# Pair blocks of the MLP: one transfer of four blocks, the first combination in place, and products in program order

## The chip, the cores and the metric

The kernel runs on one core of a Trainium2 chip. A core has a matrix engine (TensorE, PE in the profile; its weight loads are PEld), a vector engine (VectorE, DVE), an activation engine (ScalarE, ACT), a general engine (GpSimd, POOL), and a sync engine (SyncE, SP) that here only issues transfers. Each engine works through its own instructions in order and waits on semaphores for the others. Sixteen DMA engines move data. Weights come from the device memory (HBM) into the on-chip memory SBUF; TensorE adds up its products in PSUM, which has eight banks of 128 x 512 float32.

The metric is the device time of one execution in microseconds. Runs are compared by their median, and the profile is of one execution.

## What is computed

A two-layer encoder over 256 tokens of width 2048. Each layer is: normalisation, token mixing in heads, output projection, and an MLP. What the change touches is the MLP:

```python
n = rms_norm(h, mlp_norm[i])
h = h + jnp.square(jax.nn.relu(n @ w_up[i])) @ w_down[i]
```

`w_up` is 2048 x 8192 and `w_down` 8192 x 2048, all float32. TensorE works on float32r operands, so every weight tile is split into a high part (written by ScalarE) and the residual low part (VectorE subtracts). A product of two split operands is high x high, high x low and low x high: three matrix products.

## The kernel before

**Grains.** The MLP is a list of grains (`add_mlp`, line 969). A grain has a `run` (its products on TensorE), an `after`, and up to three earlier stages: `load`, `pre`, `prep`. `run_all` (line 274) walks the list; before it runs grain n it issues the loads of grains up to n + 8, the `pre` of those up to n + 5 and the `prep` of those up to n + 4 (`SOON`, line 964). This is the program order. A scheduler then orders each engine's instructions by its own estimate; instructions given to `pin` keep their program order among each other.

**Up.** The hidden width is cut into 8 parts of 8 blocks of 128. For one block (`up_grains`, line 749, two grains), SyncE loads 1 MiB of `w_up` into `raw_U`, ScalarE and VectorE split it in two halves into `uh` and `ul` (line 329 and 330), and `u_products` (line 727) makes 48 products of 256 columns into one PSUM tile `ps_u`. `squared` (line 782) then applies the ReLU (line 789) and the square (line 790) on ScalarE into `c`. For every second block VectorE forms four combinations (line 799), and the seven operands are split into `a_s`. Part 0 runs by itself; its `ps_u` tiles rotate through the four banks of the pool `ps_acc`.

**Down, by pairs.** For parts 0 to 6 the product with `w_down` is made for pairs: two hidden blocks of 128 and two column blocks of 512 at a time, with seven products in place of eight (a Strassen-like scheme with the sums p1 to p7). There are 56 such steps in a layer (`down_grains`, line 806), each beside one hidden block of the next part. The four 128 x 512 blocks of a pair come as 1024 KB: three go into tile `b` (line 814, 768 KB), the fourth into the first place of tile `t` (line 816, 256 KB). Then:

- `pre`: VectorE writes t[1] = t[0] + b[0] (line 828), and GpSimd issues a DMA that adds b[1] onto t[0] in place (line 829).
- `prep_first`: `b` (1536 columns) is split into `bh` and `bl`.
- `prep_second`: VectorE writes t[2] = t[1] + b[1] and t[3] = t[2] + b[2] (lines 837 and 838), and `t` (2048 columns) is split into `th` and `tl`.
- `run`: the products of `FIRST` (three sums, 9 products of 512 columns) use `bh` and `bl`; those of `SECOND` (four sums, 12 products) use `th` and `tl`.

`b` and `t` have two buffers each, `bh`, `bl`, `th` and `tl` one each. The seven sums stay in PSUM for eight steps at a time; when a half of the columns ends, `taken` (line 885) adds them to `h` (line 883) or to `z` (line 894), and at two places per layer `folded` combines `z` into `h`.

**PSUM.** All eight banks are in use. The pools `ps_acc` and `ps_att` (four banks each) are closed before the pairs and a pool `ps_sums` is opened, with one bank for the hidden block (tag `up`) and one for each sum. This happens in the first hidden block of part 1 (lines 763 to 768); the sums take their banks in the order p4, p3, p1, p2, p5, p7, p6 (line 871). After the pairs the pools change back.

**Plain.** Part 7 is multiplied without pairs (`plain_grains`, line 914): 1 MiB loads that alternate between the buffers with tag `U` and those with tag `T`, splits, and products into `ps_m` of `ps_acc`.

**Order of the list.** Behind part 0, each step adds four grains: first half of the hidden block, first half of the pair, second half of the hidden block, second half of the pair (line 976).

Of the kernel before, what the change touches and what calls it, by code (L numbers as in the profile page):

```python
# [10 lines left out]
F32 = mybir.dt.float32  # L11
F32R = mybir.dt.float32r
BF16 = mybir.dt.bfloat16
AF = mybir.ActivationFunctionType
ALU = mybir.AluOpType
# [75 lines left out]
def encoder_kernel(ctx: ExitStack, tc: tile.TileContext, t: dict, out: bass.AP):  # L91
# [632 lines left out]
    FIRST = ("p3", 6, 0), ("p1", 0, 1), ("p2", 2, 2)  # L724
    SECOND = ("p5", 3, 0), ("p7", 4, 1), ("p6", 5, 2), ("p4", 1, 3)

    def u_products(ps, k0, nk, hi, lo):

        acts = box["hT"]
        for j in range(nk):  # L730
            k = k0 + j
            s = slice(j * P, (j + 1) * P)
            parts = (slice(0, SEQ), slice(SEQ, 512))
            for n, x in enumerate(parts if k < KT - 1 else parts[::-1]):
                nc.tensor.matmul(ps, hi[:, s], acts[:, k, x], start=k == n == 0, stop=False)  # L735
            nc.tensor.matmul(ps, lo[:, s], acts[:, k, :SEQ], start=False, stop=k == KT - 1)  # L736
# [12 lines left out]
    def up_grains(layer, part, m):  # L749
# [8 lines left out]
        def run(hf):  # L758
            if hf == 0:
                if part == 0:  # L760
                    own["ps"] = at.acc.tile([P, 512], F32, tag="acc", name="ps_u")[:, :SEQ]
                else:
                    if part == 1 and m == 0:
                        closed("ps_att", "ps_acc")
                        at.sums = opened("ps_sums", space=bass.MemoryType.PSUM)
                        box["ps"] = {}
                        box["unused"] = set()
                    own["ps"] = at.sums.tile([P, 512], F32, tag="up", name="ps_u")[:, :SEQ]
            u_products(own["ps"], hf * (KT // 2), KT // 2, *own.pop(hf))
# [36 lines left out]
    def down_grains(layer, part, n, begins, ends):  # L806
# [4 lines left out]
        def load():  # L811
            src = t[f"w_pair{layer}"][(part * 2 + q) * STEPS + j]
            own["b"] = at.side.tile([P, 3 * 512], F32, tag="b", bufs=2, name="b")
            nc.sync.dma_start(own["b"], src[:, : 3 * 512])
            own["t"] = at.side.tile([P, 4, 512], F32, tag="T", bufs=2, name="t")
            nc.sync.dma_start(own["t"][:, 0, :], src[:, 3 * 512 :])
# [5 lines left out]
        def block(k):  # L822

            return own["b"][:, k * 512 : (k + 1) * 512]

        def pre():
            s = own["t"]
            nc.vector.tensor_tensor(s[:, 1, :], s[:, 0, :], block(0), op=ALU.add)  # L828
            nc.gpsimd.dma_start(s[:, 0, :], block(1), accum_op=ALU.add)  # L829

        def prep_first():
            own["first"] = tuple(at.mlp.tile([P, 3 * 512], F32R, tag=x, name=x) for x in ("bh", "bl"))
            split(*own["first"], own["b"])

        def prep_second():
            s = own["t"]
            nc.vector.tensor_tensor(s[:, 2, :], s[:, 1, :], block(1), op=ALU.add)
            nc.vector.tensor_tensor(s[:, 3, :], s[:, 2, :], block(2), op=ALU.add)
            own["second"] = tuple(at.mlp.tile([P, CH], F32R, tag=x, name=x) for x in ("th", "tl"))
            split(*own["second"], s.rearrange("p a b -> p (a b)"))  # L840

        def run(which, products):
            hi, lo = own.pop(which)
            a = box["a", part, j]
            for name, ai, bi in products:
# [3 lines left out]
                nc.tensor.matmul(ps, a[:, 0, ai, :], hi[:, s], start=begins, stop=False)  # L849
# [64 lines left out]
    def plain_grains(layer, nb):  # L914
# [6 lines left out]
        def load(c):  # L921
            own[c] = loaded(t[f"w_plain{layer}"][nb * 2 + c], "UT"[c])
# [46 lines left out]
    def add_mlp(layer):  # L969
        for m in range(PK):  # L970
            plan.extend(up_grains(layer, 0, m))
        for x, (p, n) in enumerate(STEPS_OF):
# [3 lines left out]
            plan.extend((up[0], down[0], up[1], down[1]))  # L976
# [304 lines left out]
```

## Time and profile before

| | |
|---|---|
| median of 3 runs | 2047.32 us (2046.8 to 2050.19) |
| the profiled execution | 2048.19 us |
| its span, first to last instruction | 2046.4 us |
| busy: PE / PEld / DVE / ACT / POOL | 2026.7 / 1813.8 / 1667.0 / 1251.6 / 119.2 us |
| read from HBM, mean | 398.17 MB, 197 GB/s |
| loads of pair blocks | 112 of 768 KB, 112 of 256 KB |

How to read the profile's lines: a group line names the source line, the engine, the operation, output<-inputs, shape and count, then busy time in us, mean ns of one, and the engine's idle time just before these instructions with what ended it. A line of a wait list gives who waited <- for whom: us in total, times, the longest. A line of the stage table gives the stretch in us from the start, its length, the busy time (and instructions) of each engine, the granted clock of PE as a share of full speed, the DMA engines' mean busy share, and GB/s. A timeline line gives the start, the duration, the instruction, and in brackets the engine's idle time before it and what released it. Lines of transfers give count, size and the median time from issue to landing. Matmul ends are modelled and overlap, so the distance between two starts is what a matmul costs.

### The profile page before, as it was taken

The numbers are of one execution on the slowest core, as the hardware profiler recorded it, in microseconds if no ns is written. First come the engines' busy times: TensorE is split into PE (matmuls) and PEld (weight loads), VectorE is DVE, ScalarE is ACT, GpSimd is POOL, SyncE is SP. The second block draws the span as 40 slices with busy tenths as digits, with TensorE's granted clock in tenths as the row PEclk, the third lists the DMA queues.
The fourth block names the chain that finished last, engine by engine and source line by source line (L and its number), as shares of the span: only waits on it lengthen the run. The fifth ranks groups of instructions, "written<-read, shape, count | busy, mean of one in ns | idle before, by whom it ended". The sixth has DMA issues, their size and how long they took to land.

```text
span 2046.4 us, 31582 instructions
## 1 busy us (share of the span) xinstructions
PE 2026.7 (99%) x12516; PEld 1813.8 (89%) x12516; DVE 1667.0 (81%) x2061; ACT 1251.6 (61%) x1652; POOL 119.2 (6%) x144
## 2 busy tenths in 40 slices
PE   8999999999999999999999999999999999999998
PEld 7888888889999999999988888889999999999996
DVE  6767667558989989999897667657998989999996
ACT  6755555556666666666656557556666666666664
POOL 0000000000000000000000001000000000000000
PEclk9999999999999999999999999999999999999999
DMA  7755554727777777787775554536877777777773
GB/s 281 283 190 179 191 177 169 277 80 233 231 231 232 220 232 230 226 242 222 230 222 199 180 185 144 184 125 216 246 227 227 227 231 229 234 232 227 236 221 130
DMA packets 93429, 433.79 MB, mean 212 GB/s; under 512 B 10464, under 2 KB 12128, under 8 KB 60128
## 3 DMA queue, kind: packets, MB, share of 16 engines
q1 hardware_dynamic: 75456, 398.47, 57.3%
q0 software_dynamic: 16816, 31.46, 8.7%
q8 instruction: 98, 1.61, 0.3%
q10 hardware_dynamic: 1008, 1.84, 0.3%
q14 instruction: 51, 0.42, 0.1%
HBM read 398.17 MB, written 4.19 MB: 197 GB/s over the span
## 4 chain that ended last, share of the span: by engine, by line
PE 93%; DVE 3%; DMA 2%; issue 1%; ACT 0%; POOLq 0%; POOL 0%; SPq 0%; DVEq 0%; ACTq 0%
PE ps_u L735 21%; PE ps_u L736 11%; PE ps_m L234 8%; PE ps_m L237 8%; PE ps_m L238 8%; PE p L849 8%; PE p L850 8%; PE p L851 8%; PE ps_s L247 7%; PE ps_s L250 3%; DMA t<-in_w_pair 1%; DVE tl L330 1%; PE pt_a L410 1%; DVE ul L330 1%; PE pt_n L347 1%
## 5 line engine op out<-in xcount | busy, mean ns | idle before, releaser
L735 PE MATMUL ps_u<-hT,uh 128*128 128x256 f32 x4096 | 713.2, 278 | 0.2
L735 PEld LDWEIGHTS ps_u<-hT,uh 128*128 128x128 f32 x4096 | 627.4, 188 | 10.3 <-ACT uh L329 0.6
L736 PE MATMUL ps_u<-hT,ul 128*128 128x256 f32 x2048 | 568.9, 278 | 1.6 <-DVE ul L330 1.5
L329 ACT ACTIVATE uh<-raw_U 128x1024 fp32r<-128x1024 f32 x278 | 294.6, 1061 | 307.1 <-PE ps_u L735 290.0
L330 DVE TENSOR_TENSOR lo<-raw,hi 128x1024 fp32r<-128x1024 f32 (+1 forms) x220 | 261.4, 1194 | 164.5 <-ACT hi L329 162.9
L736 PEld LDWEIGHTS ps_u<-hT,ul 128*128 128x128 f32 x2048 | 386.2, 189 | 4.2 <-DVE ul L330 3.2
L330 DVE TENSOR_TENSOR ul<-raw_U,uh 128x1024 fp32r<-128x1024 f32 x278 | 337.3, 1218 | 40.6 <-ACT uh L329 40.5
L329 ACT ACTIVATE hi<-raw 128x1024 fp32r<-128x1024 f32 (+1 forms) x220 | 227.5, 1039 | 210.2 <-PE ps_m L238 119.1
L329 ACT ACTIVATE th<-t 128x2048 fp32r<-128x2048 f32 x112 | 215.2, 1921 | 118.7 <-PE p L851 107.8
L330 DVE TENSOR_TENSOR tl<-t,th 128x2048 fp32r<-128x2048 f32 x112 | 256.0, 2286 | 23.9 <-ACT th L329 23.5
L330 DVE TENSOR_TENSOR bl<-b,bh 128x1536 fp32r<-128x1536 f32 x112 | 196.0, 1750 | 0.3 <-ACT bh L329 0.3
L850 PE MATMUL p<-tl,a_s 128*128 128x512 f32 x448 | 174.8, 390 | 0.0
L851 PE MATMUL p<-th,a_s 128*128 128x512 f32 x448 | 174.3, 389 | 0.0
L329 ACT ACTIVATE bh<-b 128x1536 fp32r<-128x1536 f32 x112 | 166.2, 1484 | 7.3 <-PE p L851 1.2
L829 POOL DMA_DIRECT2D t<-b x112 | 97.0, 866 | 1158.8 <-DVE t L828 556.0
L849 PE MATMUL p<-th,a_s 128*128 128x512 f32 x448 | 164.1, 391 | 0.0
L247 PE MATMUL ps_s<-nT,hi 128*128 128x512 f32 x448 | 142.5, 397 | 0.0
L851 PE MATMUL p<-bh,a_s 128*128 128x512 f32 x336 | 131.1, 390 | 0.0
L850 PE MATMUL p<-bl,a_s 128*128 128x512 f32 x336 | 131.0, 390 | 0.0
L828 DVE TENSOR_TENSOR t<-t,b 128x512 f32<-128x512 f32 x112 | 77.2, 689 | 57.6 <-DMA t<-in_w_pair 46.5
L849 PE MATMUL p<-bh,a_s 128*128 128x512 f32 x336 | 108.0, 389 | 0.0
L237 PE MATMUL ps_m<-lo,nT 128*128 128x512 f32 x264 | 103.7, 393 | 0.0
(237 smaller groups left out, 3305.1 us busy)
## 6 DMA issues: line engine op xcount, KB each, us to landing
raw_U<-in_w_up SPq DMA_DIRECT2D x128, 1024.0 KB, 6.6
b<-in_w_pair SPq DMA_DIRECT2D x112, 768.0 KB, 4.5
raw<-in_w_o SPq DMA_DIRECT2D x32, 1024.0 KB, 5.0
t<-in_w_pair SPq DMA_DIRECT2D x112, 256.0 KB, 3.4
t<-b POOLq DMA_DIRECT2D x112, 256.0 KB, 6.9
raw<-in_w_b SPq DMA_DIRECT2D x21, 1024.0 KB, 4.9
raw<-in_w_av SPq DMA_DIRECT2D x12, 1024.0 KB, 4.9
raw<-in_w_aq SPq DMA_DIRECT2D x12, 1024.0 KB, 4.9
```

Source lines behind the costliest of these rows:

```text
L234: first = nc.tensor.matmul(w.ps[i], ah, hi[:, s], start=st, stop=False)
L237: nc.tensor.matmul(w.ps[i], ah, lo[:, s], start=False, stop=False)
L238: nc.tensor.matmul(w.ps[i], al, hi[:, s], start=False, stop=sp)
L247: nc.tensor.matmul(ps, hi[:, s], acts[:, k0 + j, :], start=k0 + j == 0, stop=False)
L329: first = nc.scalar.activation(dst_hi, src, AF.Copy)
L330: return first, nc.vector.tensor_tensor(dst_lo, src, dst_hi.bitcast(F32), op=ALU.subtract)
L735: nc.tensor.matmul(ps, hi[:, s], acts[:, k, x], start=k == n == 0, stop=False)
L736: nc.tensor.matmul(ps, lo[:, s], acts[:, k, :SEQ], start=False, stop=k == KT - 1)
L829: nc.gpsimd.dma_start(s[:, 0, :], block(1), accum_op=ALU.add)
L849: nc.tensor.matmul(ps, a[:, 0, ai, :], hi[:, s], start=begins, stop=False)
L850: nc.tensor.matmul(ps, a[:, 0, ai, :], lo[:, s], start=False, stop=False)
L851: nc.tensor.matmul(ps, a[:, 1, ai, :], hi[:, s], start=False, stop=ends)
```

## The change

- The four blocks of a pair come in one transfer of 1024 KB into `b`, which now has four places (two buffers, as before). `t` has three places and is written by VectorE only; it is taken in `pre`.
- The fourth block, raw, sits in b[3]. VectorE writes t[0] = b[3] + b[0]; GpSimd's DMA then adds b[1] onto b[3] in place. The other two additions move from `prep_second` to `pre`.
- `prep_first` splits the four places of `b` (2048 columns), `prep_second` the three of `t` (1536). The sum p5 moves from `SECOND` to `FIRST`, so the groups have 12 and 9 products.
- In the list of a step the pair's first grain comes ahead of the hidden block's first grain. The closing of the old PSUM pools and the opening of `ps_sums` move from the hidden block to the first grain of the first pair.
- The first product of each group of three is pinned: in `u_products` (from part 1 on) and in the pair's `run`. Among themselves these keep their program order on TensorE.
- The plain stage's second load uses the buffers with tag `b` in place of `T`.

```diff
-    FIRST = ("p3", 6, 0), ("p1", 0, 1), ("p2", 2, 2)
-    SECOND = ("p5", 3, 0), ("p7", 4, 1), ("p6", 5, 2), ("p4", 1, 3)
+    FIRST = ("p3", 6, 0), ("p1", 0, 1), ("p2", 2, 2), ("p5", 3, 3)
+    SECOND = ("p7", 4, 0), ("p6", 5, 1), ("p4", 1, 2)
...
-    def u_products(ps, k0, nk, hi, lo):
+    def u_products(ps, k0, nk, hi, lo, keep_order=False):
...
-                nc.tensor.matmul(ps, hi[:, s], acts[:, k, x], start=k == n == 0, stop=False)
+                first = nc.tensor.matmul(ps, hi[:, s], acts[:, k, x], start=k == n == 0, stop=False)
+                if keep_order and n == 0:
+                    pin(first)
...
                 else:
-                    if part == 1 and m == 0:
-                        closed("ps_att", "ps_acc")
-                        at.sums = opened("ps_sums", space=bass.MemoryType.PSUM)
-                        box["ps"] = {}
-                        box["unused"] = set()
                     own["ps"] = at.sums.tile([P, 512], F32, tag="up", name="ps_u")[:, :SEQ]
-            u_products(own["ps"], hf * (KT // 2), KT // 2, *own.pop(hf))
+            u_products(own["ps"], hf * (KT // 2), KT // 2, *own.pop(hf), keep_order=part > 0)
...
         def load():
-            src = t[f"w_pair{layer}"][(part * 2 + q) * STEPS + j]
-            own["b"] = at.side.tile([P, 3 * 512], F32, tag="b", bufs=2, name="b")
-            nc.sync.dma_start(own["b"], src[:, : 3 * 512])
-            own["t"] = at.side.tile([P, 4, 512], F32, tag="T", bufs=2, name="t")
-            nc.sync.dma_start(own["t"][:, 0, :], src[:, 3 * 512 :])
+            own["b"] = at.side.tile([P, 4, 512], F32, tag="b", bufs=2, name="b")
+            nc.sync.dma_start(own["b"].rearrange("p a b -> p (a b)"),
+                              t[f"w_pair{layer}"][(part * 2 + q) * STEPS + j])
...
         def pre():
-            s = own["t"]
-            nc.vector.tensor_tensor(s[:, 1, :], s[:, 0, :], block(0), op=ALU.add)
-            nc.gpsimd.dma_start(s[:, 0, :], block(1), accum_op=ALU.add)
+
+            b, s = own["b"], at.side.tile([P, 3, 512], F32, tag="T", bufs=2, name="t")
+            nc.vector.tensor_tensor(s[:, 0, :], b[:, 3, :], b[:, 0, :], op=ALU.add)
+            nc.gpsimd.dma_start(b[:, 3, :], b[:, 1, :], accum_op=ALU.add)
+            nc.vector.tensor_tensor(s[:, 1, :], s[:, 0, :], b[:, 1, :], op=ALU.add)
+            nc.vector.tensor_tensor(s[:, 2, :], s[:, 1, :], b[:, 2, :], op=ALU.add)
+            own["t"] = s
...
         def prep_first():
-            own["first"] = tuple(at.mlp.tile([P, 3 * 512], F32R, tag=x, name=x) for x in ("bh", "bl"))
-            split(*own["first"], own["b"])
+            own["first"] = tuple(at.mlp.tile([P, CH], F32R, tag=x, name=x) for x in ("bh", "bl"))
+            split(*own["first"], own["b"].rearrange("p a b -> p (a b)"))
...
         def prep_second():
-            s = own["t"]
-            nc.vector.tensor_tensor(s[:, 2, :], s[:, 1, :], block(1), op=ALU.add)
-            nc.vector.tensor_tensor(s[:, 3, :], s[:, 2, :], block(2), op=ALU.add)
-            own["second"] = tuple(at.mlp.tile([P, CH], F32R, tag=x, name=x) for x in ("th", "tl"))
-            split(*own["second"], s.rearrange("p a b -> p (a b)"))
+            own["second"] = tuple(at.mlp.tile([P, 3 * 512], F32R, tag=x, name=x) for x in ("th", "tl"))
+            split(*own["second"], own["t"].rearrange("p a b -> p (a b)"))
...
         def run(which, products):
+            if part == n == 0 and which == "first":
+                closed("ps_att", "ps_acc")
+                at.sums = opened("ps_sums", space=bass.MemoryType.PSUM)
+                box["ps"] = {}
+                box["unused"] = set()
...
-                nc.tensor.matmul(ps, a[:, 0, ai, :], hi[:, s], start=begins, stop=False)
+                pin(nc.tensor.matmul(ps, a[:, 0, ai, :], hi[:, s], start=begins, stop=False))
...
-            own[c] = loaded(t[f"w_plain{layer}"][nb * 2 + c], "UT"[c])
+            own[c] = loaded(t[f"w_plain{layer}"][nb * 2 + c], "Ub"[c])
...
-            plan.extend((up[0], down[0], up[1], down[1]))
+            plan.extend((down[0], up[0], up[1], down[1]))
```

More of the change, by code (lines that the diff above doesn't have):

```diff
@@ L818, in behind @@
         def behind(fn):
             return (lambda: past(fn, box["splits"][-4])) if part == 0 and n < 2 else fn
-        def block(k):
-            return own["b"][:, k * 512 : (k + 1) * 512]
         def pre():
-            s = own["t"]
-            nc.vector.tensor_tensor(s[:, 1, :], s[:, 0, :], block(0), op=ALU.add)
-            nc.gpsimd.dma_start(s[:, 0, :], block(1), accum_op=ALU.add)
+            b, s = own["b"], at.side.tile([P, 3, 512], F32, tag="T", bufs=2, name="t")
+            nc.vector.tensor_tensor(s[:, 0, :], b[:, 3, :], b[:, 0, :], op=ALU.add)
```

## The prediction

> **What bounds the kernel now.** I read the page's first two parts, then the busy times by stage, then the waits of TensorE (PE), and last two short stretches of the timeline.
>
> ```profile
> span 2046.4 us, 31582 instructions
> PE 2026.7 (99%) x12516; PEld 1813.8 (89%) x12516; DVE 1667.0 (81%) x2061; ACT 1251.6 (61%) x1652; POOL 119.2 (6%) x144
> ```
> ```profile
> core 0: us, PE busy (x) PEld busy (x) DVE busy (x) ACT busy (x) POOL busy (x), PEclk, DMA share, GB/s
> 0.00:490.00 490.00, 481.18 (x2703) 419.40 (x2704) 327.81 (x497) 278.34 (x463) 4.46 (x11) 1.00 0.57 203
> 490.00:1066.00 576.00, 575.87 (x3863) 528.17 (x3862) 532.39 (x572) 371.45 (x375) 47.01 (x54) 1.00 0.77 230
> 1066.00:1418.00 352.00, 350.08 (x1896) 301.29 (x1895) 238.71 (x378) 207.61 (x407) 20.38 (x23) 1.00 0.49 174
> 1418.00:1994.00 576.00, 576.00 (x3869) 529.15 (x3869) 533.40 (x572) 372.29 (x376) 46.24 (x54) 1.00 0.78 231
> 1994.00:2046.00 52.00, 43.61 (x193) 35.78 (x191) 34.68 (x47) 21.94 (x33) 1.12 (x2) 0.94 0.38 137
> ```
> ```profile
> PE ps_s L247 <- DVE memT L356: 8.0, 1, 8.0
> PE ps_u L736 <- DVE ul L330: 1.5, 2, 0.8
> PE av L418 <- ACT pT L329: 1.0, 1, 1.0
> ```
>
> The change acts in the pair stage, 490 to 1066 us in layer 0 and 1418 to 1994 in layer 1 (56 steps each). There PE is busy 575.87 and 576.00 of 576 us, and the list of all that PE waits for has three rows in the whole run, none in those stages that a load or a split of a pair block causes. So the stage is bound by the products themselves, of which the change removes none: per step 48 of 256 columns and 21 of 512. VectorE (DVE) is busy 92% there and is the next bound.
>
> The sum is made on the profiled execution: 2048.19 us, 1.8 over its span, 0.87 over the median 2047.32.
>
> **The change part by part.**
>
> *Same work, other tiles.* The three additions of a step, its 3584 columns of splits and its 21x512 columns of products stay; 1536 and 2048 change places between the two halves. On PE the built program still runs 12 + 9 products back to back and then 48 for the hidden block. Cost 0.
>
> *One load instead of two; the loop that it closes.* SyncE (SP) issues 112 DMAs fewer. But a block buffer (two of them) now comes free only at the end of bl, and the built DVE order puts the first addition of the step after next, which waits for the load into that buffer, ahead of the next bl. So bl, load, one or two additions, bl must fit into one step.
>
> ```profile
> 901.07 1.92 ACT L329 ACTIVATE th<-t 128x2048 fp32r<-128x2048 f32 x1 [1.07 <-PE p L851]
> 911.32 1.92 ACT L329 ACTIVATE th<-t 128x2048 fp32r<-128x2048 f32 x1 [1.07 <-PE p L851]
> ```
> ```profile
> L330 DVE TENSOR_TENSOR tl<-t,th 128x2048 fp32r<-128x2048 f32 x112 | 256.0, 2286 | 23.9 <-ACT th L329 23.5
> L330 DVE TENSOR_TENSOR bl<-b,bh 128x1536 fp32r<-128x1536 f32 x112 | 196.0, 1750 | 0.3 <-ACT bh L329 0.3
> L828 DVE TENSOR_TENSOR t<-t,b 128x512 f32<-128x512 f32 x112 | 77.2, 689 | 57.6 <-DMA t<-in_w_pair 46.5 <-DVE ul L330 5.7 <-issue 5.2
> ```
> ```profile
> raw_U<-in_w_up SPq DMA_DIRECT2D x128, 1024.0 KB, 6.6
> b<-in_w_pair SPq DMA_DIRECT2D x112, 768.0 KB, 4.5
> raw<-in_w_o SPq DMA_DIRECT2D x32, 1024.0 KB, 5.0
> t<-b POOLq DMA_DIRECT2D x112, 256.0 KB, 6.9
> ```
>
> A step lasts 911.32 - 901.07 = 10.25 us. The 2048-column residual takes 2.29 us and an addition 0.69, so the load may take 10.25 - 2.29 - 2 x 0.69 = 6.6 us (7.3 where only one addition stands in between). No row shows a 1024 KB load of pair blocks. The ends are 5.0 us (w_o, whose queue holds little else) and 6.6 (the hidden weights, which queue behind others in this very stage). I take 5.5, nearest to the same tensor's 4.5 at 768 KB: bl ends about two residuals and an addition or two before the hidden load is issued, so the pair load goes first. That leaves 1.1 us a step; cost 0. At 6.6 it is just at the bound. What goes is DVE's wait for t, 46.5 us in all: DVE is not the bound, so it gives PE nothing. Queued behind the load's wait on SP is the next hidden load; its buffer is free two steps before its use.
>
> *t1 in place: the first split now waits for the accumulating DMA.* Before, the second split waited for it. Its wait is on ScalarE (ACT), with two hidden splits and two activations queued behind it. The built DVE order issues the addition that releases it one step before the split that needs it: 10.25 us, against 0.69 (the addition) and a landing of 6.9, so 2.7 us are left. If it came late, the split may still slip some 3 us: its residual ends about 9 us after the second group of products starts, and the products that use it start 2.04 + 10.25 = 12.3 after that. Cost 0, bound 0 to some tenths.
>
> *Where drained sums are late.* At a half's end DVE drains 4 + 3 sums instead of 3 + 4, 0.6 to 0.75 us each. Walking the built order by hand, the residual slips from 9 to at most 11 us after that start, under 12.3. Cost 0; before, the same drains cost PE no wait either.
>
> *First pair of a layer: a new wait.* The sums' pool is now opened by the first pair block, so the banks are dealt p4, p3, p1, ... and the hidden block's last; before, the hidden block took the first. The built program gives p3 the bank that the eighth hidden block of part 0 has just filled. PE's very first pair product, now held ahead of the next hidden block, waits for the ReLU that empties it, which stands on ACT behind a split that itself waits for that hidden block's last product. Before, p4 had that bank, nine products and more later.
>
> ```profile
> 489.65 0.41 PE L735 MATMUL ps_u<-hT,uh 128*128 128x256 f32 x2
> 489.89 0.39 PE L849 MATMUL p<-bh,a_s 128*128 128x512 f32 x1
> ```
> ```profile
> 489.73 1.06 ACT L329 ACTIVATE uh<-raw_U 128x1024 fp32r<-128x1024 f32 x1 [0.23 <-PE ps_u L735]
> 490.70 0.37 ACT L789 ACTIVATE c<-ps_u 128x256 f32<-128x256 f32 x1
> ```
>
> Without the two early hidden products p3 is due at 489.65; the ReLU ends at 490.70 + 0.37 = 491.07. PE stands still for 1.45 us (0.5 if ACT ran the ReLU first, 1.6 with a late wake-up). Both layers: 2.9 us. Nothing covers it: PE runs in order and all that follows is behind p3.
>
> *Last pair of a layer: a second new wait.* By the same deal the plain stage's first output tile takes p4's bank. p4 is the last sum to be finished; its drain stands on DVE behind p7's, a hidden residual and p6's. Before, that tile took the hidden block's bank, emptied by ACT beside twelve products.
>
> ```profile
> 1063.31 0.28 PE L736 MATMUL ps_u<-hT,ul 128*128 128x256 f32 x1
> 1063.43 1.09 PE L849 MATMUL p<-th,a_s 128*128 128x512 f32 x4
> 1066.17 0.39 PE L234 MATMUL ps_m<-uh,a_p 128*128 128x512 f32 x1
> ```
> ```profile
> 1063.51 1.06 ACT L329 ACTIVATE uh<-raw_U 128x1024 fp32r<-128x1024 f32 x1 [1.37 <-PE ps_u L735]
> ```
> ```profile
> 1063.63 2.35 DVE L330 TENSOR_TENSOR ul<-raw_U,uh 128x1024 fp32r<-128x1024 f32 x2
> 1065.90 1.88 DVE L894 TENSOR_TENSOR z<-p,z 128x512 f32<-128x512 f32 x3
> 1068.30 0.74 DVE L883 SCALAR_TENSOR_TENSOR h<-p,inv,h 128x512 f32<-128x512 f32 x1
> ```
>
> Twelve products take 1066.17 - 1063.43 = 2.74, so one takes 0.228 and nine take 2.05: with nine, PE is free at 1065.48. DVE: p7 is complete at about 1063.43 + 0.68 + 0.16 = 1064.27; its drain (1.88 / 3 = 0.63) ends at 1064.90, the residual (2.35 / 2) at 1066.07, p6's drain at 1066.70, p4's (0.74) at 1067.44. PE waits 1.96 us. Low end 0.9 (p4's drain alone and the wake-up), high end 3.0 (DVE still late from the fold). Both layers: 3.9 us.
>
> *Given back.* PE's idle in these stages is 0.13 us, so at most a few tenths; I take 0.3.
>
> Sum: 2.9 + 3.9 - 0.3 = 6.5 us. 2048.19 + 6.5 = 2054.7 on the profiled execution, 2053.8 on the median. With the ends, 2 x (0.5 + 0.9) = 2.8 to 2 x (1.6 + 3.0) = 9.2: 2050.1 to 2056.5.
>
> **The rivals.**
>
> *The load loop binds (slower by more).* It decides where the pair load lands later than 6.6 us after bl. For it: the hidden weights' 6.6 and a DMA share of 0.77 in this stage. Against: the 4.5 us of the same tensor. At 6.8 us it costs 0.2 x 112 = 22 us on top of the edges: 2053.8 + 22 = 2076. Chance 0.11.
>
> *The edge waits are not there (no change).* A wait that ACT or DVE clears sooner than my walk says, or idle made up for: 2047 to 2051. For it: before, the same two engines never held PE in the pair stages. Against: both tiles now follow directly on the work that frees their bank. Chance 0.12.
>
> *The pinned order shortens the step (faster).* It decides from 4.1 / 112 = 0.037 us a step, with the edge waits absent too. For it: the two hidden products before the first pair product take 489.89 - 489.65 = 0.24 us against 0.228 for one of twice the width, so a change between the two kinds of products may cost 0.012 us, and a step has two. Against: the order still has both changes, and 10.25 us is 21 x 0.228 and 48 x 0.114, so nothing else is there to gain. Were the step 0.05 us shorter, twice what both changes cost: 2047.3 - 5.6 = 2041.7. Chance 0.04. The Trainium skill ("DMA: Bandwidth & Descriptors", Anatomy of one DMA) speaks for a gain: each DMA has a fixed cost of about 2.0 us, so 112 fewer would spare some 224 us of latency by that estimate; by that rule the sum stays, since the trace shows this latency as DVE's wait of 46.5 us and PE with no wait for it.
>
> *A stall lowers TensorE's clock (slower).* The stages with PE busy have a clock of 1.00, the last one 0.94, 52 x 0.06 = 3.1 us lost. Were each of the four waits to cost as much: 2053.8 + 12.4 = 2066. Against: PE's 1.0 us wait for pT left the clock of its stage at 1.00. Chance 0.03. The rule that speaks for it is the Trainium skill's ("TensorE: Matmul & The Clock Gate", Part 1): the clock falls to half after an idle window of about 3.4 us; by it waits of 2 us would mostly not suffice, and this trace shows no wait between 1.0 and 8.0 us to test it.
>
> **How the numbers follow.** Forecast 0.70, the rivals 0.11, 0.12, 0.04, 0.03. 0.2% of this time, 4.1 us, is about what a measurement of this kernel can tell from no change: slower is above 2051.4. Of the forecast's 0.70, 0.05 lies below that (low ends together). Slower 0.65 + 0.11 + 0.03 = 0.79, same 0.05 + 0.12 = 0.17, faster 0.04. The forecast's own range is 2050 to 2057; to hold 8 in 10 I take 2048 to 2064, which leaves out the faster case, part of the no-change case and most of the load loop.
>
> **What would show it.** In the changed profile: PE's list of waits gets p on the ReLU's c (about 1.45 us, twice) and ps_m on the drained h (about 2 us, twice), and these alone. PE is again near 100% busy between; a step is 10.25 us by two th rows; the load of b lands in 5 to 6 us; DVE's first addition waits little for it; the first split waits little for the accumulating DMA. Wrong if a step is longer than 10.25 us (load or accumulation late), if PE waits at each half's end, or if the four edges are shorter than 0.5 and 0.9 us.

## The result, and the profile after

The changed kernel takes 2067.11 us (median of 4 runs, 2063.13 to 2069.32) beside 2048.76 us for the kernel before on the same chip (2046.8 to 2051.72): a ratio of 1.0086, 95% interval 1.0064 to 1.0108. It is slower, as forecast, but by some 18 us in place of 6.5, outside the range. The profiled execution took 2068.6 us.

The page's head, then the stage table, of the kernel after:

```profile
span 2066.8 us, 31484 instructions
PE 2032.5 (98%) x12516; PEld 1817.5 (88%) x12516; DVE 1673.6 (81%) x2061; ACT 1255.7 (61%) x1652; POOL 119.1 (6%) x144
```
```profile
core 0: us, PE busy (x) PEld busy (x) DVE busy (x) ACT busy (x) POOL busy (x), PEclk, DMA share, GB/s
490.00:1066.00 576.00, 574.21 (x3867) 527.53 (x3865) 532.64 (x570) 372.29 (x372) 47.01 (x54) 1.00 0.74 230
...
1418.00:1994.00 576.00, 568.51 (x3803) 521.38 (x3802) 528.53 (x564) 369.98 (x371) 47.15 (x55) 0.99 0.74 228
1994.00:2066.00 72.00, 62.13 (x309) 52.26 (x308) 49.30 (x60) 31.30 (x45) 1.12 (x2) 0.94 0.40 144
```

The span grew by 20.4 us and PE's busy time by 5.8 alone. The list of all that PE waits for had three rows before. It now begins:

```profile
PE ps_u L739 <- DVE ul L330: 8.0, 6, 2.0
...
PE ps_m L234 <- DVE h L881: 3.8, 2, 1.9
PE p L847 <- ACT c L787: 2.6, 2, 1.3
PE p L848 <- DVE bl L330: 1.8, 1, 1.8
...
```

The second and third rows are the two forecast edges. The first was 1.5 us before, and the last is new; below it two rows of 0.2 us each are new as well. Between the edges nothing changed: the rows of two steps in the middle of layer 0, the transfers, and what ScalarE (ACT) and VectorE (DVE) wait for in DMAs:

```profile
906.13 1.49 ACT L329 ACTIVATE th<-t 128x1536 fp32r<-128x1536 f32 x1 [0.39 <-PE p L849]
916.38 1.49 ACT L329 ACTIVATE th<-t 128x1536 fp32r<-128x1536 f32 x1 [0.39 <-DVE t L824]
```
```profile
b<-in_w_pair SPq DMA_DIRECT2D x112, 1024.0 KB, 5.0
...
b<-b POOLq DMA_DIRECT2D x112, 256.0 KB, 3.4
```
```profile
ACT bh L329 <- DMA b<-b: 16.1, 6, 6.9
```
```profile
DVE t L821 <- DMA b<-in_w_pair: 11.0, 8, 3.0
```

A step is still 916.38 - 906.13 = 10.25 us. The load of four blocks lands after 5.0 us, DVE waits 11.0 us for it in all (46.5 before), and ACT's first split waits for the accumulating DMA in only 6 of 112 steps, 16.1 us in all.

I measured PE's lost time as the distance between the starts of two matmuls less what the earlier one costs (0.114 us for 256 columns, 0.227 for 512), so that products slowed by a lower clock count as lost time too. By stretches of the run, after less before: 450 to 500 us +6.0, 1050 to 1100 +1.6, 1400 to 1450 +8.0, from 1950 to the end +7.4, and elsewhere -2.3 (of which -2.1 between 700 and 1050). So all of it lies at the two ends of the two pair stages.

**The start of a pair stage.** Timeline of the kernel after, about the first pair of layer 0: the addition on DVE that releases the accumulating DMA, then ACT, DVE and PE.

```profile
474.89 0.68 DVE L821 TENSOR_TENSOR t<-b 128x512 f32<-128x512 f32 x1
```
```profile
479.28 0.37 ACT L787 ACTIVATE c<-ps_u 128x256 f32<-128x256 f32 x1
...
481.14 1.92 ACT L329 ACTIVATE bh<-b 128x2048 fp32r<-128x2048 f32 x1 [1.05 <-DMA b<-b]
```
```profile
483.09 2.29 DVE L330 TENSOR_TENSOR bl<-b,bh 128x2048 fp32r<-128x2048 f32 x1 [1.73 <-ACT bh L329]
485.30 1.22 DVE L330 TENSOR_TENSOR ul<-raw_U,uh 128x1024 fp32r<-128x1024 f32 x1
```
```profile
484.06 0.50 PE L736 MATMUL ps_u<-hT,uh 128*128 128x256 f32 x2
486.58 0.39 PE L739 MATMUL ps_u<-hT,ul 128*128 128x256 f32 x1 [2.01 <-DVE ul L330]
```

The same rows of the kernel before:

```profile
479.16 1.47 ACT L329 ACTIVATE bh<-b 128x1536 fp32r<-128x1536 f32 x1
```
```profile
480.66 1.76 DVE L330 TENSOR_TENSOR bl<-b,bh 128x1536 fp32r<-128x1536 f32 x1 [0.15 <-ACT bh L329]
482.34 1.22 DVE L330 TENSOR_TENSOR ul<-raw_U,uh 128x1024 fp32r<-128x1024 f32 x1
```

Here the pair's split stands ahead of a hidden residual (ul) that PE needs at once. That residual begins at 485.30 in place of 482.34, 2.96 us later. The largest part is the accumulating DMA: it landed at 481.12, and bh starts at 481.14, where ACT was free for it at 479.28. Of these 1.86 us two activations fill some 0.8, and ACT idles for 1.05. The longer bh and bl (2048 columns in place of 1536) add 0.45 and 0.53, and 0.12 us is an offset that this kernel's timeline has already at the hidden split ahead of them (478.31 in place of 478.19). PE stands still for 2.18 us. Waits of 0.2 us and more of this kind add up to 3.0 us in layer 0 and 4.9 in layer 1.

**The end of layer 1's pair stage.** First DVE, with the addition ahead of the accumulating DMA of the last pair but one, then that DMA's issue on POOL, then ACT, DVE and PE:

```profile
1975.22 0.69 DVE L821 TENSOR_TENSOR t<-b 128x512 f32<-128x512 f32 x1
```
```profile
1977.11 0.86 POOL L822 DMA_DIRECT2D b<-b  x1 [14.82 <-DVE z L905]
```
```profile
1984.25 1.92 ACT L329 ACTIVATE bh<-b 128x2048 fp32r<-128x2048 f32 x1 [6.93 <-DMA b<-b]
```
```profile
1986.20 2.29 DVE L330 TENSOR_TENSOR bl<-b,bh 128x2048 fp32r<-128x2048 f32 x1 [3.15 <-ACT bh L329]
```
```profile
1988.55 0.50 PE L848 MATMUL p<-bl,a_s 128*128 128x512 f32 x1 [1.82 <-DVE bl L330]
```

The DMA was issued at 1977.11, 1.89 us after the addition had started; the profile names as its releaser an instruction of the fold (z, L905) that stands behind the addition. A load of hidden weights was issued at 1977.68, and the DMA landed at 1984.09: 6.98 us. In layer 0 its counterpart was issued 1.22 us after the addition had started and 1.2 us ahead of the load, landed in 3.99 us, and PE did not wait. With 0.34 us on the product before, PE loses 2.4 us here.

**The clock.** Windows of the kernel after; the third column from the right is PE's granted clock:

```profile
core 0: us, PE busy (x) PEld busy (x) DVE busy (x) ACT busy (x) POOL busy (x), PEclk, DMA share, GB/s
484.33:487.74 3.41, 1.40 (x12) 1.19 (x12) 3.41 (x4) 3.38 (x5) 0.00 (x0) 1.00 0.57 151
487.74:491.15 3.41, 3.36 (x17) 3.06 (x15) 3.41 (x4) 0.80 (x2) 0.88 (x1) 0.50 0.93 291
...
1419.58:1422.99 3.41, 1.63 (x14) 1.63 (x15) 3.41 (x4) 3.06 (x5) 0.10 (x1) 1.00 0.53 149
1422.99:1426.41 3.42, 1.42 (x14) 1.23 (x12) 3.42 (x5) 1.06 (x1) 0.80 (x1) 1.00 0.83 242
1426.41:1429.82 3.41, 3.41 (x16) 3.41 (x17) 3.38 (x6) 0.00 (x0) 0.86 (x1) 0.50 0.74 233
```

At 487.74, 1426.41, 1989.61 and 2013.50 us PE ran for 3.41 us at half clock; the kernel before had no such stretch until its products were over. Each costs 3.41 / 2 = 1.7 us, 6.8 in all. Each comes within 4 us of a wait of about 2.1 us; the waits of 2.07 us at 1069.76 and of 2.18 us at 1419.07 set off none.

### The profile page after: what moved, and what is told of

The parts are those of the page before. It is cut to its first block, busy times and chain, and to the rows that moved or that the text cites. A ratio compares the mean times of both kernels' runs of the same rounds, so it can differ in the third digit from the quotient of the medians.

```text
span 2066.8 us, 31484 instructions
## 1 busy us (share of the span) xinstructions
PE 2032.5 (98%) x12516; PEld 1817.5 (88%) x12516; DVE 1673.6 (81%) x2061; ACT 1255.7 (61%) x1652; POOL 119.1 (6%) x144
## 3 DMA queue, kind: packets, MB, share of 16 engines
q10 hardware_dynamic: 1008, 1.84, 0.3%
## 4 chain that ended last, share of the span: by engine, by line
PE 95%; DVE 1%; DMA 1%; issue 1%; ACT 1%; POOLq 0%; POOL 0%; SPq 0%; ACTq 0%; DVEq 0%
PE ps_u L736 22%; PE ps_u L739 11%; PE p L847 9%; PE p L848 8%; PE p L849 8%; PE ps_m L234 8%; PE ps_m L237 8%; PE ps_m L238 8%; PE ps_s L247 7%; PE ps_s L250 3%; DMA b<-b 1%; PE pt_a L410 1%; DVE ul L330 1%; PE pt_n L347 1%; PE av L418 0%
## 5 line engine op out<-in xcount | busy, mean ns | idle before, releaser
L736 PEld LDWEIGHTS ps_u<-hT,uh 128*128 128x128 f32 x4096 | 629.4, 189 | 10.3 <-ACT uh L329 1.2
L329 ACT ACTIVATE bh<-b 128x2048 fp32r<-128x2048 f32 x112 | 215.3, 1922 | 116.8 <-PE p L849 85.9
L330 DVE TENSOR_TENSOR bl<-b,bh 128x2048 fp32r<-128x2048 f32 x112 | 256.3, 2288 | 17.2 <-ACT bh L329 17.2
L330 DVE TENSOR_TENSOR tl<-t,th 128x1536 fp32r<-128x1536 f32 x112 | 196.7, 1756 | 40.8 <-ACT th L329 39.5
L329 ACT ACTIVATE th<-t 128x1536 fp32r<-128x1536 f32 x112 | 166.7, 1488 | 38.7 <-PE p L849 37.9
L847 PE MATMUL p<-bh,a_s 128*128 128x512 f32 x448 | 175.1, 391 | 2.8 <-ACT c L787 2.6
L848 PE MATMUL p<-bl,a_s 128*128 128x512 f32 x448 | 174.9, 390 | 1.8 <-DVE bl L330 1.8
L849 PE MATMUL p<-bh,a_s 128*128 128x512 f32 x448 | 175.2, 391 | 0.0
L822 POOL DMA_DIRECT2D b<-b x112 | 97.0, 866 | 1156.8 <-DVE t L821 965.5
L847 PE MATMUL p<-th,a_s 128*128 128x512 f32 x336 | 131.4, 391 | 0.0
L848 PE MATMUL p<-tl,a_s 128*128 128x512 f32 x336 | 131.2, 390 | 0.0
L849 PE MATMUL p<-th,a_s 128*128 128x512 f32 x336 | 130.7, 389 | 0.0
L238 PE MATMUL ps_m<-hi,nT 128*128 128x512 f32 x264 | 103.2, 391 | 0.0
```

Of the source, the lines that this page charges most:

```text
L238: nc.tensor.matmul(w.ps[i], al, hi[:, s], start=False, stop=sp)
L329: first = nc.scalar.activation(dst_hi, src, AF.Copy)
L330: return first, nc.vector.tensor_tensor(dst_lo, src, dst_hi.bitcast(F32), op=ALU.subtract)
L736: first = nc.tensor.matmul(ps, hi[:, s], acts[:, k, x], start=k == n == 0, stop=False)
L822: nc.gpsimd.dma_start(b[:, 3, :], b[:, 1, :], accum_op=ALU.add)
L847: pin(nc.tensor.matmul(ps, a[:, 0, ai, :], hi[:, s], start=begins, stop=False))
```

## The experiments

All kernels were run beside the kernel before, whose medians were 2047.27, 2047.26 and 2047.79 us in the three sessions. "Stall" is time lost by PE by the distance of starts.

**The banks dealt anew (e1_banks).** The kernel after, with the banks dealt so that p3 and the plain stage's first tile get banks that are long free.

```diff
-            for x in ("p4", "p3", "p1", "p2", "p5", "p7", "p6"):
+            for x in ("p4", "p6", "p7", "p3", "p1", "p2", "p5"):
...
+                box["up0"] = at.sums.tile([P, 512], F32, tag="up", name="ps_u")
```

> The changed kernel with the PSUM banks dealt otherwise: the hidden block's tile takes bank 0 first, then p4, p6, p7, and p3, p1, p2, p5 the four banks of the attention pool. Theory: the loss of some 20 us is a sum of four parts: bank waits at the edges (2 x 1.4 and 2 x 2.1 us), hidden residuals late at each layer's first pairs (7.9 us), a late residual at the end of layer 1 (2.4 us), and four stretches of 3.4 us at half clock that such stalls set off (4 x 1.7 us). This kernel should lose the edge waits and the half-clock stretch behind layer 1's last pair: 2057 to 2061, and PE's list of waits without p on c and ps_m on h. Rival (the edges hide other late work that then shows): 2063 to 2067, with new or longer waits of PE in the list.

2057.37 us (2057.28 to 2057.98), ratio 1.0044 (1.0029 to 1.0058). The first rows of PE's list of waits, without the row of memT:

```profile
PE ps_u L739 <- DVE ul L330: 6.5, 6, 2.0
PE p L850 <- DVE bl L330: 1.8, 1, 1.8
```

Both edge waits are gone, and with the last of them one of the four stretches at half clock: 7.1 + 1.7 = 8.8 us of the 9.7 gained. The edges were what the prediction said. They are about half of the loss, counted with that stretch; 10.1 us over the kernel before are left (2057.37 beside 2047.27).

**The order alone (e2_order).** The kernel before with the order of the change (program order held on PE, the sums' pool opened by the first pair, the first pair block ahead of the hidden one), but with its own two loads and t1 beside t.

```diff
-            plan.extend((up[0], down[0], up[1], down[1]))
+            plan.extend((down[0], up[0], up[1], down[1]))
```

> The kernel before with the order alone: pinned products, the pair's first grain ahead of the hidden block's, and the pools opened there; loads, tiles and additions as before. Theory: the bank waits at the edges (about 6.5 us) and little else, with 0 to 2 half-clock stretches: 2055 to 2059. Rival (the late residuals at the first pairs come from the order too): 2063 to 2067. Rival (the order costs nothing): 2048.

2056.52 us (2054.03 to 2057.87), ratio 1.0039 (1.0026 to 1.0052). PE's list without the row of memT begins:

```profile
PE ps_m L234 <- DVE h L885: 5.5, 2, 3.1
PE p L851 <- ACT c L786: 2.6, 2, 1.3
PE ps_u L738 <- DVE ul L330: 2.2, 4, 0.8
PE p L852 <- DVE tl L330: 2.2, 2, 1.7
```

The edge waits come with the order and the pool, not with the tiles. The hidden residual, 8.0 us of waits after the whole change, is at 2.2 here. No stretch at half clock came.

**The tiles alone (e3_tiles).** The kernel after without its order: nothing held on PE, the old list order and pool opening.

```diff
-            plan.extend((down[0], up[0], up[1], down[1]))
+            plan.extend((up[0], down[0], up[1], down[1]))
...
-                pin(nc.tensor.matmul(ps, a[:, 0, ai, :], hi[:, s], start=begins, stop=False))
+                nc.tensor.matmul(ps, a[:, 0, ai, :], hi[:, s], start=begins, stop=False)
```

> The changed kernel without the order: one transfer of four blocks, t1 in place, 12 and 9 products, but no pins, the hidden block first and the pools opened as before. Theory: no bank waits at the edges; the first split still waits for the accumulating DMA at each layer's first pairs and delays the hidden residuals behind it by up to 2 us: 2052 to 2058. Rival (the tiles are harmless once TensorE's order is free): 2048.

2066.21 us (2065.68 to 2066.45), ratio 1.0086 (1.0071 to 1.0101): a miss, and the most telling one. The part that was costed at nothing loses as much as the whole change. The two parts do not add up: the tiles alone cost 18.9 us, the order alone 9.3, both together 18 to 20 by the medians.

```profile
PE ps_u L739 <- DVE ul L330: 8.9, 4, 3.7
...
PE ps_u L736 <- ACT uh L329: 2.8, 2, 1.7
PE p L847 <- ACT bh L329: 2.1, 1, 2.1
```

There are no edge waits; there are stalls of 3.84 us at the first pairs of both layers, each with 6.83 us at half clock behind it, and one of 2.29 us at the end of layer 1.

**The first pairs' preparation placed later (e4_behind).** The kernel after, with the whole preparation of the first two pairs (additions, accumulating DMA and splits) behind the newest hidden split rather than the fourth newest.

```diff
-            return (lambda: past(fn, box["splits"][-4])) if part == 0 and n < 2 else fn
+            return (lambda: past(fn, box["splits"][-1])) if part == 0 and n < 2 else fn
```

> The changed kernel with the preparation of a layer's first two pairs held three hidden splits later (behind the latest split in place of the fourth from last), so that the first pair's split, which waits for its accumulating DMA, no longer stands ahead of the hidden split on ScalarE and VectorE. Theory: the waits of the hidden products at the first pairs (7.9 us in all) and one or two half-clock stretches go: 2056 to 2061. Rival (VectorE has too much work there whatever its order): the wait moves to the pair's residual and the time stays at 2064 to 2068.

2068.99 us (2068.1 to 2072.02), ratio 1.0102 (1.0087 to 1.0117); the theory's figure was missed. The rival is nearer, 1 us beyond its range: the wait moves.

```profile
PE p L847 <- ACT c L787: 6.2, 2, 3.2
PE p L848 <- DVE bl L330: 4.3, 3, 1.8
...
PE ps_u L739 <- DVE ul L330: 1.5, 2, 0.8
```

The hidden residual is in time again (1.5 us, as before the change), and the pair's own products wait instead, for their residual (bl) and for the ReLU (c) that empties p3's bank. So in neither of the two places is there room for this preparation at a layer's start.

**The first pair prepared earlier (e5_early).** The banks dealt anew, and at a layer's start the additions and the accumulating DMA put two grains earlier.

```diff
+    EARLY = (8, 7, 4)
...
+        soon = EARLY if part == 0 or part == 1 and m == 0 else SOON
```

> The kernel with the banks dealt anew (2057.4 us), and the first pair's additions and its accumulating DMA put two grains earlier at the start of each layer. Theory (the first split waits for the accumulating DMA, and the hidden residual stands behind it on VectorE): the DMA lands some 5 us earlier, the first split starts up to 1.4 us earlier, the stalls of 2.18 us at the first pairs shrink to 0.8 us or less, and their two half-clock stretches of 3.41 us do not come: 2.8 + 3.4 = 6.2 us off, 2051 us (2049 to 2053). Rival (the longer splits of four blocks, 1.92 and 2.29 us, make the stall whatever the DMA does): the stalls stay at 2.1 us or more, 2056 to 2058 us. In either case the stall of 2.1 us near the end of layer 1 stays.

2052.01 us (2050.55 to 2052.57), ratio 1.0020 (1.0011 to 1.0029), inside the theory's range, though its mechanism holds only in part. The split of layer 0's first pair on ACT, and the row of the hidden residual in PE's list (6.5 us with the banks alone):

```profile
475.20 1.90 ACT L329 ACTIVATE bh<-b 128x2048 fp32r<-128x2048 f32 x1
```
```profile
PE ps_u L739 <- DVE ul L330: 5.6, 6, 1.7
```

The DMA lands at 474.43, and bh starts right behind a hidden split; the stall at the first pair shrinks from 2.18 to 0.57 us, and neither layer has a stretch at half clock there. But the stall at the second pair grew from 0.6 and 0.8 us (layers 0 and 1) to 1.8 us: DVE runs without a gap from 477.13 to beyond 488 us, and PE, no longer slowed ahead of it, comes to that wait earlier. So PE's waits for ul shrink by 0.9 us only, and most of the 5.4 us gained is the two stretches. By the distance of starts PE loses 11.2 us about the first pairs (475 to 500 and 1400 to 1440 us) with the banks alone, 6.0 here, and 2.4 in the kernel with the same order and banks but the tiles of before (e6_order_banks). The DMA's wait, with the half clock that came of it, was thus the larger part of this cause; the longer splits and the additions on DVE are the rest, and how much of it is each was not taken apart.

**Some accumulations on VectorE (e7_vec).** The banks dealt anew, and for five pairs of a layer (the first and the last four) DVE adds in place of the DMA.

```diff
+            if part == n == 0 or part == PARTS - 2 and n >= STEPS:
+                nc.vector.tensor_tensor(b[:, 3, :], b[:, 3, :], b[:, 1, :], op=ALU.add)
```

> The kernel with the banks dealt anew (2057.4 us), and five of the 56 accumulations of a layer (the first pair's and those of the last four pairs) done by VectorE in place of the DMA. Theory: at the first pairs as with the earlier DMA, 5 to 6 us off; near the end of layer 1 the first split starts when the addition is done, some 1.1 us earlier than with the DMA (which took 6.9 us there), the stall shrinks from 2.1 to about 1 us and its half-clock stretch of 3.41 us goes, 2.8 us off: 2049 us (2047.5 to 2052). Rival (VectorE's 0.69 us more per pair is paid by PE, since VectorE is busy 187 of 200 us): 2053 to 2058 us.

2054.8 us (2054.56 to 2057.92), ratio 1.0036 (1.0023 to 1.0049): the rival's figure. At the first pairs the stalls fell to 0.96 and 1.53 us. At the end of layer 1 the stall stayed at 2.13 us although bh, which no longer waited for a DMA, was done at 1975.94: bl began only at 1977.79, behind additions and the fold's instructions on DVE. In layer 0 a stall of 2.70 us was new. So at that place DVE's queue alone is enough for a stall of this size.

**The fold placed later (e10_fold).** As with the earlier preparation, and the fold of the first half of the columns, seven instructions of DVE, put behind the splits of the plain stage.

```diff
+                if box.pop("fold_later", False):
+                    past(lambda: folded(0), box["splits"][-4])
```

> The kernel with the banks dealt anew and the earlier preparation at the first pairs (2052.0 us), and the fold of the first half of the columns (seven instructions of VectorE per layer) put behind the splits of the plain stage. Theory (near the end of a layer the fold's instructions stand ahead of the additions on VectorE, so that the accumulating DMA of a late pair is issued late and runs beside a load, 6.9 us, and TensorE waits 2.1 us and then runs a window at half clock): that wait and its stretch go, 2.8 + 1.7 us off, 2047.5 us (2046 to 2050). Rival (the fold's 4.9 us are then late for the plain stage, which waits for banks that VectorE has yet to drain): 2050 to 2055 us.

2050.9 us (2049.14 to 2054.09), ratio 1.0015 (1.0006 to 1.0024): 0.9 us outside the theory's range and inside the rival's, and against the earlier preparation alone (1.0011 to 1.0029) the gain of 1.1 us is not clear of the noise. The rival's waits for banks are not in PE's list. In layer 1 the stall is gone, and no stretch at half clock comes before the products are over. In layer 0 a stall of 1.66 us appeared at the same place, and it is a DMA's. The split of layer 0, then that of layer 1:

```profile
1043.11 1.92 ACT L329 ACTIVATE bh<-b 128x2048 fp32r<-128x2048 f32 x1 [6.15 <-DMA b<-b]
```
```profile
1979.85 1.92 ACT L329 ACTIVATE bh<-b 128x2048 fp32r<-128x2048 f32 x1 [1.06 <-PE p L852]
```

Layer 0's accumulating DMA was issued at 1033.67, 1.1 us after a pair load and 2.4 us ahead of a hidden load, and took 9.27 us. So the fold made it late in layer 1; what the DMA takes beside loads is a second condition.

**The tiles of before, the order of the change, the banks dealt anew (e6_order_banks, e11_best).** One kernel, measured twice; its edit is that of the banks on top of that of the order alone.

> The kernel before, with the order of the change (program order held on TensorE, pool opened at the first pair) and the banks dealt anew, but with the tiles of before (two loads, t1 beside t). Theory (the order alone cost bank waits, the rest of the change's cost is the tiles'): the waits of 1.47 x 2, 3.22 and 2.59 us that the order alone showed (2056.5 us) go, 8.8 us off; 2047.7 us (2046.5 to 2050), no half-clock stretch. Rival (holding the order costs in itself): 2052 us or more.

> The tiles of before with the order of the change and the banks dealt anew, measured once more and longer (2045.75 us, ratio 0.9991 from 0.9981 to 1.0 at first). Theory (with the bank waits gone the held order saves the 0.2 us per 50 us that the products of before lose in some stretches, about 1.5 us): 2045.5 us, ratio 0.9992 and an interval that ends below 1. Rival (no difference): 2046.5 to 2048 us.

2045.75 us (2044.66 to 2047.25, 10 runs), ratio 0.9991 (0.9981 to 1.0); then 2045.76 us (2043.93 to 2048.23, 11 runs), ratio 0.9987 (0.9978 to 0.9996). PE's list in the second, without the row of memT, begins:

```profile
PE ps_u L738 <- DVE ul L330: 2.2, 4, 0.8
...
PE p L854 <- DVE tl L330: 0.5, 1, 0.5
```

The held order costs nothing once the banks are right; with the second interval just below 1 (the first reaches it) it saves some 2 us. This is the fastest kernel of the case, and it has neither the one load nor t1 in place. Between it and the kernel with the banks dealt anew (2057.37) only the tiles differ: they cost 11.6 us.

**The clock by itself (e8_stalls, e9_longer).** To the kernel just described, in 28 steps, a forced wait: ACT writes a block of th once more, with the same values, between two products that read it; once, and then four times over.

```diff
+                again = which == "second" and at_n == 1 and n % 4 == 1
+                if again:
+                    nc.scalar.activation(hi[:, s], own["t"][:, bi, :], AF.Copy)
```

> As the kernel with the order and the banks, and in 28 steps (every fourth) a block of the second split is written once more by ScalarE (same values) between two products that read it, so that TensorE waits for ScalarE's queue, 0.8 to 2.7 us each by ScalarE's instructions (a copy of 512 columns, behind an activation of up to 1.9 us): 2047.7 + 28 x 1.5 = 2090 us (2070 to 2125). Theory of the clock (windows of 3.413 us that lie on one grid over the whole run; a window in which TensorE idles for more than about 2.0 us is followed by one at half clock; the windows of the six traces so far divide between 1.89 us, full, and 2.07 us, half): each window with 2.07 us of idle or more is followed by a half-clock window and no other, so stalls of the same length set it off or not by where they fall. Rival (a single wait of about 2 us or more sets it off wherever it falls): each wait above 2.1 us is followed by a half-clock stretch.

> As the kernel with 28 forced waits, but ScalarE writes the block four times in place of once, so that the forced wait of 0.84 us grows by three copies of some 0.52 us to about 2.4 us, the same length at 28 places. Theory of the clock (windows of 3.413 us on one grid over the whole run, half clock after a window with more than about 2.05 us of idle): a wait of 2.4 us puts that much into one window from about half of the places that it can fall on, so some 14 of the 28 (9 to 19) are followed by a half-clock stretch, each from the end of its window, and which ones follows from the grid. Rival (a wait of more than 2.1 us sets it off wherever it falls): all 28. Time: 2046 + 28 x 2.4 + 14 x 1.7 + what VectorE is late by after each (36 us in the kernel with the short waits) = 2173 us (2140 to 2230).

With one copy (2105.47 us, one run) the forced wait was 0.84 us each time, with waits for tl behind it (16.9 us in PE's list, the longest 2.8). Ten windows had 1.00 to 1.83 us of idle and none of them was followed by half clock; the one with 3.10 us was. With four (2215.9 us, one run) the wait was not 2.4 but 3.4 to 4.0 us, since each copy waited for the one before it, so the count of 14 was missed: 27 of the 28 were followed by a stretch at half clock. The one that was not is the test of the two theories. Timeline and windows of the kernel with four copies:

```profile
1568.89 0.39 PE L858 MATMUL p<-tl,a_s 128*128 128x512 f32 x1
1572.80 0.50 PE L859 MATMUL p<-th,a_s 128*128 128x512 f32 x1 [3.52 <-ACT th L857]
```
```profile
1567.61:1571.02 3.41, 1.67 (x10) 1.12 (x8) 1.93 (x5) 2.93 (x6) 0.00 (x0) 1.00 0.64 220
1571.03:1574.44 3.41, 1.64 (x7) 1.38 (x8) 1.17 (x2) 1.72 (x3) 0.00 (x0) 1.00 0.90 296
1574.44:1577.85 3.41, 3.41 (x23) 3.02 (x22) 1.76 (x3) 3.01 (x2) 0.84 (x1) 1.00 0.23 88
```

A wait of 3.68 us, longer than the waits of 2.1 us that brought the clock down in the kernel after, fell across a border of the grid, 1.91 us in one window and 1.89 in the next, and the clock stayed at 1.00. One such case would be little, but the order alone (e2_order) has two more: waits of 3.21 and 2.59 us, 1.45 and 1.84 us of idle time in the two windows of the first and 1.68 and 0.99 in those of the second, and no stretch at half clock behind either.

## Why the prediction missed

On the profiled execution 2054.7 us was predicted and 2068.6 measured. The 13.9 us: +10.3 for waits behind the first split (7.9 at the first pairs, 2.4 at layer 1's end), +6.8 for the clock, +0.3 for the edges, and -3.5 as the remainder: 2.3 is the time gained outside the ends of the stages, and the rest was not traced.

*What bounds the kernel, same work in other tiles, step of 10.25 us.* Right.

*One load instead of two.* Right: it lands after 5.0 us, half a microsecond under the 5.5 taken, the step did not grow, and DVE's wait for t went from 46.5 to 11.0 us without any gain for PE. So the latency that fewer DMAs were to spare, some 224 us by the estimate, was worth nothing to PE; the section of the Trainium skill that the estimate goes by is on DMAs that GpSimd issues, while these loads are SyncE's. The rival of the load loop is out.

*t1 in place.* This step failed: "2.7 us are left. If it came late, the split may still slip some 3 us ... Cost 0, bound 0 to some tenths". It was walked for a step in the middle of the stage, and there it costs PE nothing. Even there the margin was thinner than said: the split starts a median of 8.8 us after the addition, not 10.25, and the DMA is issued 1.2 us after the addition starts, not 0.69, so that the landing of 6.9 us that was taken would have left 0.7 us in place of 2.7. The landing fell to 3.4 us, which was not foreseen, and that is luck.

The step was not walked at the first pairs. There ACT is free for the split 4.4 us after the addition has started (474.89 to 479.28), while the addition, the issue and a landing of 4.86 us take 6.2; and bh and bl stand on ACT and DVE ahead of hidden residuals that PE needs within a microsecond, so that the split may slip by nothing like 3 us. Nor was it walked at the last pairs, where the fold's instructions stand among the additions, so that the DMA was issued late, beside a load, and landed in 6.98 us. The tiles alone show that the loss is theirs (2066.21 us for a part that should have cost nothing). The cost was 10.3 us of waits, and the clock on top. Of the 11.6 us that the tiles cost with the right banks, the earlier preparation takes away 5.4 and the later fold 1.1 more; how the 5.1 us that are left divide between the longer splits, the additions and the DMA stays open.

*Drained sums late at a half's end.* No PE wait stands at the ends of the halves in the middle of the stage. Right.

*First pair, p3's bank.* 1.45 us predicted; PE's starts at 494.08 and 495.67 give 1.59 - 0.114 = 1.47, in both layers. *Last pair, p4's bank.* 1.96 predicted, 2.07 in both layers. Mechanism and size were right, and dealing the banks anew took both away. The rival without edge waits is out.

*Given back.* 0.3 taken. The held order gives back more: by the kernel with the tiles of before and the right banks, 2.0 us of its median. The rival that the pinned order shortens a step does not hold as put: the step is 10.25 us still, and the gain comes from the small losses that the products of before have in some stretches (0.6 us between 750 and 800, for one).

*A stall lowers the clock.* Given 0.03, and it came true, at 1.7 us a stretch rather than 3.1. The 3.1 was read from a stage in which the half clock came only after the last product (2037.22 us, the clock fell at about 2040), so it was no cost of a stall. The rival's 2066 us lies near the measured time by luck. Its reason against, the clock of 1.00 about a wait of 1.0 us, was no evidence on a wait of 2 us. Of the four forecast waits only one set it off; the other three stretches came from the waits that were not foreseen. Its setting off hangs on where a wait falls, so it may also make part of the spread of 6 us between the runs of the kernel after. Their mean granted clocks fit: 0.995 for 2069.32 and 2068.6 us, 0.996 for 2065.61, 0.997 for 2063.13. A mean lower by 0.002 is 0.004 of the run at half clock, and half of that lost, some 4 us. Only one of these runs has a trace, so which waits made the difference is not shown.

"These alone" in what would show it was thus wrong in two large rows of PE's list, the hidden residual's and bl's.

## What to carry to other kernels

A cover that is worked out for a steady step has to be worked out once more at the first and the last steps of the stage, where other work stands in the same queues: here all the loss of 20 us lay in the first and last few of 112 steps. When a DMA's result moves to an earlier consumer, ask what stands behind that consumer on its engine, and count the time from what releases the DMA to that consumer at each of these places: the landing of 6.9 us taken here was hardly exceeded, the cover was shorter than thought. When pools are opened in another order, deal the banks by hand so that the first tile of the next stage gets one that is long free.

## What the runs showed of the hardware that was not expected

*The clock goes by windows on a grid.* In each run the stretches at half clock begin at multiples of 3.413 us from one another (in the kernel after 275, 165 and 7 of them apart) and last one such window, or two. I took that grid through the 13 traces of this case (the kernel before, the one after, and the eleven runs) and summed PE's idle time, by the distance of starts, in each window between 30 us and the end with 1 us of it or more, without those that were at half clock themselves: 113 windows. In 70 the idle time was 1.00 to 2.04 us, and the next window was at full clock in every one; in 43 it was 2.07 us or more, and the next was at half clock in every one. So the bound lies between 2.04 and 2.07 of 3.413 us of idle time, 60%. The Trainium skill ("TensorE: Matmul & The Clock Gate", Part 1) describes a free-running activity window of 4096 cycles, about 3.4 us, which the grid agrees with; its rule that the clock falls after an idle window of that length does not fit here if it is read as a window without work: 2.07 us of idle in a window are enough. That 3.68 us across a border are not agrees with a rule by windows.

*The accumulating DMA.* 256 KB from SBUF to SBUF landed in a median of 6.9 us in the kernel before, with two pair loads and a hidden load a step, and of 3.4 us in the kernel after, with one of each. In the kernel after it ranged from 3.2 to 7.0 us, in the one with the later fold to 9.3. What makes it long was not tested. A load of 1 MB close by is not enough: in the kernel after, 74 of the 76 DMAs that landed within 3.6 us had one issued within 2.5 us of them, though none within 1.3. The one of 7.0 us had one 0.56 us behind it, the one of 9.3 us had one 1.1 us ahead and another 2.4 us behind.

*The size of a load.* With 1024 KB in one transfer the load of a pair took a median of 5.0 us in the kernel after, where 768 KB had taken 4.5 in the kernel before.
